# New durations and waits in a kernel's own list scheduler, and a stricter page allocator

## The chip, the cores and the metric

The kernel runs on one core of one Trainium2 chip. The metric is the device time of one execution in microseconds (us), lower being better. A core has five engines that work side by side, each through a queue of its own: the tensor engine (PE, whose weight loads the profile lists as PEld), the vector engine (DVE), the scalar engine (ACT), GpSimd (POOL) and the sync engine (SP), which here issues all DMA transfers. An engine takes its instructions in the order in which they were queued and waits on semaphores for the others.

## The reference

One inference step of a one-layer network, for 1024 prompt tokens and 32 sample tokens of width 1024, in float32:

```python
def layer(x, mk, mv, hg_s0, rw_s0, shift0, lb, lw):
    n = rmsnorm(x, lw['norm_mix'])
    p = n @ lw['w_in']
    hg_o, hg_s = hgrn2_mixer(p[..., :HG_COLS], lb, lw['hgrn_norm'], hg_s0)
    rw_o, rw_s, rw_shift = rwkv7_mixer(p[..., HG_COLS:], shift0, rw_s0, ...)
    x = x + jnp.concatenate([hg_o, rw_o], axis=-1) @ lw['w_out']
    x = x + cross_attend(rmsnorm(x, lw['norm_cross']), mk, mv, lw['w_cq'], lw['w_co'])
    n = rmsnorm(x, lw['norm_ffn'])
    x = x + (jax.nn.silu(n @ lw['w_ff1']) * (n @ lw['w_ff3'])) @ lw['w_ff2']
    return x, hg_s, rw_s, rw_shift
```

The HGRN2 mixer (4 heads of 128) and the RWKV-7 mixer (8 heads of 64) are recurrences over the tokens. The memory's keys and values, `rmsnorm(mem) @ w_k` and `@ w_v` for 256 memory tokens, are computed as well and returned, as are the states of the mixers. A last RMSNorm gives the outputs.

## The kernel before, in words

The 1056 tokens lie along the free dimension in three blocks of 352 (`TB`), the features on the partitions. Every weight and every activation of a dense product is split into two float32r parts, high and low; a product is the sum of three (high x high, high x low, low x high). `load_w` loads a column tile of a weight (128 x 1024, 512 KB), multiplies it by a norm's gain on DVE, and makes the parts, the high one on ACT and the low one on DVE or, for the mixers' projections, on POOL. `gemm` does the products of such a tile, 24 for each block of 352 tokens, into a bank of PSUM.

In the mixers (`mixers`, `rwkv`, `hgrn`) the tokens are worked through in segments of 256, in chunks of 64 or blocks of 32. There the products are small (64 or 128 columns, float32 or float16), and each piece is a long chain from engine to engine: PE, then ACT or DVE, then PE. `inverse`, which inverts triangular 64 x 64 matrices for RWKV-7, makes ACT copy float16 results between small products. The projections `x @ w_in` are the work that PE can do while such a chain is under way.

Nothing of this is issued as it stands in the code. Every call of an engine is recorded as a node of a graph by `Graph.record`, with edges from the reads and writes of the tiles, and a line of products on PE makes one node (`gemm` cuts it after six products). Then `Graph.order`, a list scheduler, plans all engines on the host while the program is built:

- `price` gives the time that a node takes on its engine and how much later its result can be used; `wait` gives the time from one engine's result to its use by another; `change` is added when PE goes from one node to another.
- A node's priority is the longest path of prices and waits from it to the end of the graph. A node may carry a bias that pushes it back (`BIAS`): the projections have it, so they fill in where nothing else is ready.
- For every engine a clock is kept. The engine that could start first gets, of its nodes whose operands are there by then and whose new tiles have a place (`fits`), the one with the longest path.
- `FIFO` names kinds of tiles that must be placed in the order of recording, and how many of each may live; `AHEAD` says how many units (an RWKV piece `rw`, its chain `rc`, an HGRN piece `hg`, a piece of attention `at`) may be under way at once; `LEAD` says when one of six phases may open.
- SBUF is given out in units of 66 words of a partition, in pages of 16 units, in five regions (`REGIONS`). "F" regions hold ordinary tiles, "R" regions float32r operands. In the mixers the regions f0, mb and ma (192, 192 and 64 units) are F, and hold all ordinary tiles, the projections' results among them. `place` looks for the place that is free the earliest; `fits` asks whether there is one; `take` gives it out. `RESERVE` units (64 in the mixers) are kept for the oldest node that is still to be issued.

The planned order is then issued as it is, engine by engine, and the hardware waits wherever a result is later than planned. The pick itself is this loop:

```python
for t, n in sorted(ready[e], key=lambda r: (max(r[0], now), -r[1].path)):
    t = max(t, now)
    if pick is not None and t >= pick[0]:
        break
    s = fits(n, t)
    if s is None:
        continue
    if pick is None or s < pick[0]:
        pick = s, n
    if s <= now:
        break
...
if e == "tensor":
    n.cost += change(last, n)
```

All instructions are issued from one line of `emit` (L337 in the profile), so the profile is read by the names of tiles. These are the regions: f, mb, ma are F regions (mb and ma become R later), r and wr hold float32r operands and raw weights, bank is PSUM.

## Time and profile before

| | |
|---|---|
| time, median of 3 runs | 2035.69 us (2035.36 to 2036.48) |
| profiled execution, span from first to last instruction | 2034.7 us |
| instructions | 36538 |
| busy: PE | 1954.2 us (96%), 14417 products |
| busy: DVE | 1101.1 us (54%) |
| busy: ACT | 801.0 us (39%) |
| busy: POOL | 622.5 us (31%) |
| DMA | 100.59 MB, mean 49 GB/s |

The profiled execution has its span as its own time; its device time isn't listed apart, and the median of the runs is 1.0 us above it. PE is busy nearly all the time, so the time is that of PE's products plus the idle time of PE plus what a lowered clock costs. The granted clock of PE is a share of its full speed: at 0.5 products take twice as long. A row of the table by stages has the length of the stretch, the busy time of each engine in it with its number of instructions, the granted clock, the share of the DMA engines and GB/s. A row of the waits says which engine waited, for whom, the total in us, how often, and the longest. A row of the groups has operation, tiles, shapes and number, then busy time in us and mean ns of one, then the idle time before.

### The profile page before, as it was taken

To read this page: it belongs to the slowest core of one execution; us is meant where nothing else is said; L and a number is where in the kernel's file an instruction comes from. 1 tells how busy PE (TensorE), PEld (TensorE's weight loads), DVE (VectorE), ACT (ScalarE), POOL (GpSimd) and SP (SyncE) were. 2 spreads that over 40 slices of the span, in tenths; PEclk is the share of its full clock that TensorE was granted. 3 is DMA by queue.
4 is the path that set the end of the run, shared out by engine and by line. 5 is a ranking of instruction groups with operands and counts; after the bars stand their busy time and mean duration, and the time that the engine had idled before them with its cause. 6 is when DMAs were issued, how large, how long until landed. Compare 5 with 4: busy or idle time off the path is not lost.

```text
span 2034.7 us, 36538 instructions
## 1 busy us (share of the span) xinstructions
PE 1954.2 (96%) x14417; PEld 1813.2 (89%) x14417; DVE 1101.1 (54%) x2584; ACT 801.0 (39%) x2066; POOL 622.5 (31%) x954
## 2 busy tenths in 40 slices
PE   7989999998999899899999999999999999999998
PEld 6878777787877788899989999999999999999997
DVE  4876677768767766635754356333333344323345
ACT  4576546845765676633332233121111112111122
POOL 4742343334434331206300056230022233310221
PEclk8999999998999999899999999999999999999999
DMA  4100100011010101541211111111211111111112
GB/s 139 42 22 25 35 23 27 23 34 33 22 32 18 33 23 58 179 147 42 73 42 42 42 53 42 42 40 40 59 50 39 40 58 42 50 40 53 46 42 86
DMA packets 159115, 100.59 MB, mean 49 GB/s; under 512 B 7776, under 2 KB 153824, under 8 KB 158944
## 3 DMA queue, kind: packets, MB, share of 16 engines
q1 hardware_dynamic: 158944, 98.26, 16.0%
q8 instruction: 113, 1.85, 0.4%
q14 instruction: 58, 0.48, 0.1%
HBM read 86.69 MB, written 11.55 MB: 48 GB/s over the span
## 4 chain that ended last, share of the span: by engine, by line
PE 59%; DVE 4%; POOL 1%; ACT 1%; issue 1%; DMA 1%; SPq 0%; DVEq 0%; ACTq 0%
PE bank L337 59%; DVE f L337 2%; ACT f L337 1%; POOL f L337 1%; DVE r L337 1%; POOL r L337 1%; DVE mb L337 0%; ACT mb L337 0%; DMA wr<-in_w_ck_dram 0%; ACT r L337 0%; DMA f<-mix_scratch 0%; DMA wr<-in_w_cq_dram 0%; DVE wr L337 0%; SPq L337 0%; POOL mb L337 0%
## 5 line engine op out<-in xcount | busy, mean ns | idle before, releaser
L337 PE MATMUL bank<-r 128*128 128x352 f32 x5904 | 1040.1, 331 | 12.4 <-POOL r L337 5.3
L337 PEld LDWEIGHTS bank<-r 128*128 128x128 f32 x5904 | 955.1, 190 | 27.6 <-POOL r L337 5.8
L337 DVE TENSOR_TENSOR f<-bank,f 128x256 f16<-128x256 f32 (+9 forms) x689 | 252.6, 391 | 355.4 <-PE bank L337 339.8
L337 PE MATMUL bank<-mb,r 128*128 128x352 f32 (+3 forms) x2448 | 411.5, 325 | 4.6 <-DVE r L337 2.5
L337 PEld LDWEIGHTS bank<-mb,r 128*128 128x128 f32 x2448 | 396.1, 188 | 9.5 <-DVE r L337 4.3
L337 POOL TENSOR_TENSOR f<-f 128x352 f32<-128x352 f32 (+6 forms) x242 | 198.2, 835 | 482.0 <-ACT f L337 459.4
L337 PE MATMUL bank<-f 128*128 128x64 f16 (+7 forms) x2612 | 291.6, 253 | 35.2 <-DVE f L337 15.7
L337 ACT CAST r<-wr 128x1024 fp32r<-128x1024 f32 (+2 forms) x154 | 145.1, 946 | 311.8 <-PE bank L337 298.1
L337 ACT ACTIVATE f<-f 128x256 f32<-128x256 f32 (+5 forms) x372 | 147.0, 411 | 245.9 <-DVE f L337 217.7
L337 PEld LDWEIGHTS bank<-f 128*128 128x128 f32 (+4 forms) x1564 | 163.6, 162 | 66.8 <-DVE f L337 16.9
L337 ACT COPY f<-f 64x256 f16<-64x256 f16 (+1 forms) x408 | 149.1, 367 | 46.1 <-DVE f L337 37.8
L337 DVE TENSOR_TENSOR r<-wr,r 128x1024 fp32r<-128x1024 f32 (+2 forms) x124 | 142.1, 1150 | 43.5 <-ACT r L337 43.3
L337 DVE TENSOR_TENSOR wr<-wr,f 128x1024 f32<-128x1024 f32 x82 | 105.8, 1292 | 104.5 <-DMA wr<-in_w_ff_dram 89.1
L337 POOL TENSOR_TENSOR r<-f,r 128x352 fp32r<-128x352 f32 x48 | 62.3, 1312 | 271.1 <-DVE f L337 216.9
L337 POOL TENSOR_SCALAR f<-f 128x64 f32<-128x64 f32 (+6 forms) x124 | 54.7, 442 | 159.2 <-DVE f L337 100.0
L337 DVE TENSOR_TENSOR ma<-bank,ma 128x352 f32<-128x352 f32 (+6 forms) x96 | 45.3, 486 | 94.6 <-PE bank L337 84.1
L337 PEld LDWEIGHTS <-f 128*128 128x128 f16 x1156 | 52.5, 99 | 35.6 <-issue 8.2
L337 POOL TENSOR_TENSOR r<-wr,r 128x1024 fp32r<-128x1024 f32 x30 | 71.7, 2393 | 29.5 <-ACT r L337 25.9
L337 ACT CAST mb<-f 128x352 fp32r<-128x352 f32 x66 | 30.9, 484 | 123.0 <-DVE f L337 114.7
L337 PE MATMUL bank<-f,mb 64*64 64x64 f32 (+7 forms) x830 | 75.3, 250 | 1.4 <-DVE f L337 1.1
L337 ACT ACTIVATE f<-bank,f 128x256 f32<-128x256 f32 (+4 forms) x122 | 51.1, 432 | 56.4 <-DVE f L337 19.7
L337 DVE TENSOR_TENSOR f<-bank,r 128x352 f32<-128x352 f32 x60 | 30.4, 518 | 77.0 <-PE bank L337 77.0
(167 smaller groups left out, 1770.6 us busy)
## 6 DMA issues: line engine op xcount, KB each, us to landing
wr<-in_w_ff_dram SPq DMA_DIRECT2D x44, 512.0 KB
wr<-in_w_in_dram SPq DMA_DIRECT2D x30, 512.0 KB
wr<-in_w_ff_dram SPq DMA_DIRECT2D x24, 384.0 KB
f<-mix_scratch SPq DMA_DIRECT2D x24, 176.0 KB
mb<-in_x_prompt_dram SPq DMA_DIRECT2D x16, 256.0 KB
wr<-in_w_ck_dram SPq DMA_DIRECT2D x8, 512.0 KB
wr<-in_w_cv_dram SPq DMA_DIRECT2D x8, 512.0 KB
wr<-in_w_out_dram SPq DMA_DIRECT2D x8, 512.0 KB
```

The lines of the kernel that those rows point to most:

```text
L337: getattr(eng, method)(*args, **kw)
```

## The change

It changes the planner alone; the recorded network is the same. `price` gets other durations, above all longer ones for ACT, POOL and DMA, longer ones for float32r products and other ones for small float32 products. `wait` becomes a table by producing and consuming engine. `change` is now 0.095 us wherever the size of the part of the array in use changes (rows up to 64 or not, columns up to 64 or not), and 0 elsewhere. `place` gets a rule: a node that isn't the oldest may not put an ordinary tile into an empty page where fewer than two pages are empty. `fits` now tries the places of all new tiles of a node one after the other, largest first, with the earlier ones taken, instead of each by itself. The tiles "raw" and "mixed" (the projection before and after the token shift in RWKV, 352 columns) come into `FIFO` with four live each. All comments and descriptions are removed as well.

```diff
-WAIT, WAIT_PE, SWITCH = 0.0, 0.1, 0.06
+SWITCH = 0.095
-FIFO = {"wr": 2, "wh": 2, "wl": 2, "p": 44, "h": 12, "rp": 5, "wr2": 4, "wh2": 8, "wl2": 8, "ckv": 7, "mrow": 2}
+FIFO = {"wr": 2, "wh": 2, "wl": 2, "p": 44, "h": 12, "rp": 5, "wr2": 4, "wh2": 8, "wl2": 8, "ckv": 7, "mrow": 2, "raw": 4, "mixed": 4}
...
+WAIT = {("vector", "tensor"): 0.2, ("vector", "gpsimd"): 0.18, "vector": 0.115, ("scalar", "tensor"): 0.1,
+        ("scalar", "gpsimd"): 0.05, "scalar": 0.02, ("gpsimd", "tensor"): 0.08, "gpsimd": 0.0, "tensor": 0.21,
+        ("sync", "tensor"): 0.08, "sync": 0.0}
 def wait(a, b):
-    if a == b:
-        return 0.0
-    if b == "tensor":
-        return 0.2 + WAIT_PE
-    return {"tensor": 0.2, "gpsimd": 0.08}.get(a, 0.14) + WAIT
+    return 0.0 if a == b else WAIT.get((a, b), WAIT[a])
 def price(eng, method, args, kw):
     if method == "dma_start":
-        return 0.45 + n * out.shape[0] * 4 / 380e3, 1.2
+        return max(0.4, n * out.shape[0] * 4 / 200e3), 1.9
     if eng == "tensor":
         if method == "transpose":
-            return (0.056 if args[1].shape[0] == 64 else 0.109), 0.0
+            return (0.056 if args[1].shape[0] <= 64 else 0.109), 0.0
         lhs = kw["lhsT"]
-        m = math.prod(lhs.shape[1:])
+        k, m = lhs.shape[0], math.prod(lhs.shape[1:])
         if lhs.dtype == F16:
-            return 0.029, 0.0
+            return max(0.029, n / 2400 + 0.002), 0.0
         if lhs.dtype == F32R:
-            return (n if n >= 256 else 4 * n) / 2400 + 0.002, 0.0
-        return (n / 790 if m == 64 else 4 * n / 2400 + 0.003), 0.0
+            return (n if n >= 256 else 4 * n) * 0.4375e-3 + 0.007, 0.0
+        if k <= 64 and m <= 64:
+            return max(0.03, n * 0.92e-3), 0.0
+        if k <= 64:
+            return max(0.112, n * 1.25e-3), 0.0
+        if m <= 64:
+            return (0.059 if n >= 64 else 0.112), 0.0
+        return max(0.223, n / 600 + 0.005), 0.0
     if eng == "vector":
         if method == "tensor_reduce":
             n = math.prod(args[1].shape[1:])
-        return 0.065 + n * 1.04e-3 + (0.065 if method in ("scalar_tensor_tensor", "tensor_tensor_scan") else 0.0), 0.0
-    if method == "affine_select":
-        return 0.3, 0.0
-    if method == "memset":
-        return 0.04 + n * 0.5e-3, 0.0
+        if method == "tensor_tensor_scan":
+            return 0.07 + n * 2.08e-3, 0.0
+        return 0.065 + n * 1.05e-3 + (0.065 if method == "scalar_tensor_tensor" else 0.0), 0.0
     if eng == "scalar":
-        return 0.095 + n * 0.83e-3 + (0.06 if any(isinstance(kw.get(k), View) for k in ("scale", "accum_out")) else 0.0), 0.0
+        pointer = any(isinstance(kw.get(k), View) for k in ("scale", "bias", "accum_out"))
+        return (0.18 if args[1].buf.space == "PS" else 0.21) + n * 0.83e-3 + (0.095 if pointer else 0.0), 0.0
+    if method == "affine_select":
+        return 0.35, 0.0
+    if method == "memset":
+        return 0.06 + n * 0.5e-3, 0.0
     if method == "tensor_tensor":
-        return 0.1 + n * 2.1e-3 + (0.45 if args[3] == ALU.pow else 0.0), 0.0
+        return 0.22 + n * 2.2e-3 + (0.45 if args[3] == ALU.pow else 0.0), 0.0
     if method == "tensor_scalar":
-        return 0.2 + n * (2.6e-3 if args[4] == ALU.max else 1.1e-3), 0.0
-    return 0.1 + n * 1e-3, 0.0
+        return 0.3 + n * (2.9e-3 if args[4] == ALU.max else 1.3e-3), 0.0
+    return 0.24 + n * 1e-3, 0.0
...
+def cut_of_array(call):
+    method, args, kw = call
+    op = args[1] if method == "transpose" else kw["lhsT"]
+    return op.shape[0] <= 64, method != "transpose" and math.prod(op.shape[1:]) <= 64
 def change(a, b):
-    if a is None:
-        return 0.0
-    (_, x, kx), (m, y, ky) = a.calls[-1], b.calls[0]
-    if m == "transpose":
-        full, half = y[1].dtype == F32, False
-    else:
-        full = ky["lhsT"].dtype != F16
-        half = math.prod(ky["lhsT"].shape[1:]) == 64
-    if math.prod(x[0].shape[1:]) > 64 or not full:
-        return 0.003
-    return 0.033 if half else SWITCH
+    return SWITCH if a is not None and cut_of_array(a.calls[-1]) != cut_of_array(b.calls[0]) else 0.0
...
-        def place(b, start):
+        def place(b, start, first):
             units = b.units
             step = 16 if units > 12 else 4 if units > 2 else units
             free = np.where(pages(b), freed, BIG)
             if units <= 16:
                 cand = free.reshape(-1, 16)
                 idle = (cand < BIG).sum(1)
+                if not first and b.kind == "F" and b.cls not in HOME and (idle == 16).sum() < 2:
+                    cand = np.where(idle[:, None] == 16, BIG, cand)
...
         def fits(n, start):
             first = n.i == oldest
...
-                for b in sb:
-                    if b.at is None:
-                        at = place(b, start)
-                        if at is None:
-                            return None
-                        start = max(start, at[1])
+                tried = []
+                for b in sorted(sb, key=lambda b: -b.units):
+                    at = place(b, start, first)
+                    if at is None:
+                        break
+                    start = max(start, at[1])
+                    lo, hi = at[0], at[0] + b.units
+                    tried.append((lo, hi, freed[lo:hi].copy()))
+                    freed[lo:hi] = BIG
+                for lo, hi, was in reversed(tried):
+                    freed[lo:hi] = was
+                if len(tried) < len(sb):
+                    return None
             return start
...
-                got = place(b, start)
+                got = place(b, start, n.i == oldest)
```

More of the change, by code (lines that the diff above doesn't have):

```diff
@@ L442, in place @@
                 idle = (cand < BIG).sum(1)
-                best = None
+                if not first and b.kind == "F" and b.cls not in HOME and (idle == 16).sum() < 2:
+                    cand = np.where(idle[:, None] == 16, BIG, cand)
                 offs = range(0, 17 - units, step)
```

## The prediction

> **What bounds the kernel now.** I read the table by stages first, cut where the kinds of work change: start, mixers, the step from the mixers to the output projection, and the dense products. Then came the waits of the tensor engine (PE) in the mixers.
>
> ```profile
> core 0: 2034.7 us, clock 0.978
> ```
>
> ```profile
> 0.00:100.00 100.00, 82.59 (x524) 76.00 (x526) 60.84 (x126) 51.59 (x125) 59.15 (x137) 0.91 0.29 92
> 100.00:800.00 700.00, 659.41 (x6400) 552.80 (x6397) 492.46 (x1468) 441.00 (x1293) 263.80 (x508) 0.97 0.10 28
> 800.00:1000.00 200.00, 187.70 (x1227) 180.38 (x1226) 115.06 (x206) 92.57 (x211) 67.54 (x82) 0.96 0.35 107
> 1000.00:2034.70 1034.70, 1024.48 (x6278) 1004.01 (x6277) 432.71 (x786) 215.89 (x440) 231.97 (x228) 1.00 0.16 49
> ```
>
> The columns after the length are busy time of PE, its weight loads, DVE, ACT and POOL, then the granted clock. PE is idle for 17.4, 40.6, 12.3 and 10.2 us, 80.5 us in all. The mean clock of 0.978 costs up to 0.022 x 2034.7 = 44.8 us more: 9 at the start (0.09 x 100), 21 in the mixers (0.03 x 700), 8 in the step (0.04 x 200). What an order can win is in these two sums. They overlap where PE stands idle at half clock, so 125 us is a ceiling. The dense half has little to give: one of its slices shows PE without a gap.
>
> ```profile
> 1300.00:1400.00 100.00, 100.00 (x623) 100.00 (x622) 33.67 (x50) 18.25 (x32) 26.05 (x24) 1.00 0.15 43
> ```
>
> That is 100 / 623 = 0.1605 us for one product of 352 columns. The old price is 352/2400 + 0.002 = 0.149 us, the new one 352 x 0.0004375 + 0.007 = 0.161 us. The new price is right, and the product stays as long as it was.
>
> Who ends the waits of PE in the mixers (total, number, longest):
>
> ```profile
> PE bank L337 <- DVE f L337: 14.5, 18, 2.5
> PE bank L337 <- ACT mb L337: 7.1, 9, 1.9
> PE bank L337 <- ACT f L337: 6.7, 12, 2.2
> PE bank L337 <- DVE mb L337: 4.6, 2, 4.2
> PE bank L337 <- DVE ma L337: 3.0, 2, 1.9
> PE bank L337 <- ACT ma L337: 2.3, 4, 1.1
> ```
>
> DVE ends 14.5 + 4.6 + 3.0 = 22.1 us, ACT 7.1 + 6.7 + 2.3 = 16.1 us. In these places the planner put a product in PE's queue before its operand was there, and everything behind it waits, since PE takes its products in order.
>
> **The change part by part.** No instruction is added or removed: the same products, copies and DMAs are put in another order and at other addresses. So the arithmetic costs the same, and only waits, the clock, and interference between engines can move. The new prices against the trace:
>
> ```profile
> L337 ACT COPY f<-f 64x256 f16<-64x256 f16 x320 | 128.0, 402 | 37.1 <-DVE f L337 30.2 <-POOL f L337 1.4
> L337 POOL TENSOR_TENSOR f<-f 128x352 f32<-128x352 f32 x138 | 148.4, 1100 | 391.1 <-ACT f L337 389.8
> L337 POOL TENSOR_TENSOR r<-wr,r 128x1024 fp32r<-128x1024 f32 x30 | 71.7, 2393 | 29.5 <-ACT r L337 25.9 <-PE bank L337 3.2
> L337 DVE TENSOR_TENSOR r<-wr,r 128x1024 fp32r<-128x1024 f32 x84 | 110.7, 1318 | 40.6 <-ACT r L337 40.5
> L337 DVE TENSOR_TENSOR f<-f,r 128x352 f32<-128x352 f32 x48 | 37.0, 784 | 1.0
> ```
>
> ACT's copy of 256 columns: old 0.307, new 0.422, traced 0.402. POOL's sum of 352: old 0.839, new 0.994, traced 1.100; its subtraction of 1024: old 2.250, new 2.473, traced 2.393. DVE's subtraction of 1024: old 1.130, new 1.140, traced 1.318; its sum of 352: old 0.431, new 0.435, traced 0.784. So ACT and POOL come to within a tenth, and DVE stays short by 14 to 45%.
>
> **ACT's waits** (16.1 us). A run of such copies was planned a quarter too short (0.307 for 0.402), so PE's operand came later than planned. With the new price the planner issues a projection product in the meantime, which is ready whenever its weights are. I take two thirds away, 10.7 us; a third stays since the allowance from ACT to PE falls as well, from 0.30 to 0.10. Bounds: all 16.1 gone, or 8 more.
>
> **DVE's waits** (22.1 us). The price is the old one, and the longest wait shows why it falls short. Rows of DVE, POOL and PE in order of time:
>
> ```profile
> 645.18 2.34 POOL L337 TENSOR_TENSOR r<-wr,r 128x1024 fp32r<-128x1024 f32 x1
> 645.25 2.48 DVE L337 TENSOR_TENSOR f<-mb,ma 128x192 f32<-128x192 f32 x1 [0.67 <-POOL mb L337]
> 648.41 0.97 PE L337 MATMUL bank<-mb 64*128 64x128 f32 x5 [4.25 <-DVE mb L337]
> ```
>
> A DVE operation priced at 0.065 + 192 x 0.00105 = 0.267 us lasts 2.48 us, as long as POOL's subtraction beside it. The Trainium skill, in "SBUF — State Buffer" under "Who interferes with whom", says that a DVE instruction with two SBUF inputs contends with a GpSimd instruction that reads SBUF, and that the second to issue blocks until the first has finished; this row agrees. No price by shape holds that, before or after. I take no change here. Bounds: half gone (-11) by the truer times of the other engines, or doubled (+22), by the rival below.
>
> **The clock.** One short wait and what followed:
>
> ```profile
> 145.60:147.50 1.90, 0.10 (x3) 0.05 (x2) 1.86 (x8) 0.00 (x0) 1.76 (x4) 1.00 0.00 0
> 151.20:158.10 6.90, 6.90 (x54) 5.35 (x55) 2.79 (x11) 1.58 (x4) 1.35 (x4) 0.51 0.00 0
> ```
>
> PE is busy for 0.10 of 1.90 us, and 3.7 us later runs 6.9 us at 0.51. So a wait costs clock as well: 21 / 40.6 = 0.52 us for each us of idle time in the mixers. With the 10.7 us go 5.5 us. The Trainium skill ("TensorE: Matmul & The Clock Gate", "What's actually happening") puts the throttle after at least one idle window of about 3.4 us. By that alone, the shorter waits would cost no clock and the 5.5 us would drop out of the sum; this row, a throttle after a wait of under 2 us, speaks for keeping them.
>
> **The step from mixers to output projection** (12.3 us idle). Here late loads stand in the chain that ended last:
>
> ```profile
> 861.85 5.77 DMA wr<-in_w_ck_dram
> 883.88 4.53 DMA f<-mix_scratch
> ```
>
> The waits of PE in this stage:
>
> ```profile
> PE bank L337 <- DVE f L337: 5.2, 4, 3.2
> PE bank L337 <- DVE r L337: 4.2, 5, 1.3
> PE bank L337 <- ACT mb L337: 1.8, 1, 1.8
> ```
>
> A weight of 512 KB was planned at 1.83 + 1.2 = 3.03 us and is now at 2.62 + 1.9 = 4.52; the traced piece is 5.77. The scratch load goes from 2.12 to 2.80, the piece is 4.53. Waits on r and mb behind such loads are 4.2 + 1.8 = 6.0 us; I take half away, 3.0 us, and with it clock at 8 / 12.3 = 0.65, 2.0 us. Bounds: all 6.0, or nothing. SP only issues these loads, which are no later in its queue for being priced higher.
>
> **The start** (17.4 us idle):
>
> ```profile
> PE bank L337 <- DMA f<-in_norm_mix_dram: 6.8, 1, 6.8
> PE bank L337 <- POOL r L337: 5.3, 2, 5.0
> PE bank L337 <- DVE mb L337: 3.2, 1, 3.2
> ```
>
> The first wait is for the first parameters and is not the planner's. The second is POOL's weight subtraction behind constants; its price hardly moves. I take nothing; bounds 5 less, 3 more.
>
> **Allocator and rest.** The exact trial of several tiles and the order imposed on "raw" and "mixed" (four live each) cost nothing while look-ahead has room. Free-kind SBUF in the mixers is 192 + 192 + 64 units, 28 pages of 16, and the rule keeps one empty page back from all but the oldest node. What hides it is the other 27; if that cover goes, it is a rival. The price of a switch (0.095) and the lower price of short products (0.059 for 0.081) move only the planner's clock, since the pick is made before the switch is added.
>
> The sum: 10.7 + 5.5 + 3.0 + 2.0 = 21.2 us less. The profiled span is 2034.7 us against a median of 2035.69, about 1 us outside it that stays. 2035.7 - 21.2 gives 2014.5, say 2014 us.
>
> **The rivals.**
>
> *More is won:* all ACT waits (16.1), half of DVE's (11), clock on both (27.1 x 0.52 = 14), the step (6 + 4), the start (5): 56 us, 1980 us. For it: every long wait is a planning error. Against it: DVE's price.
>
> *DVE's waits grow, slower.* The old planner allowed 0.30 us from any engine to PE, the new one 0.20 from DVE, so the cushion that covered a short DVE price shrinks by 0.10 us at each crossing, while PE's products are no longer priced short, which had given DVE time too. DVE has 1468 instructions in the mixers. If its waits double, 22.1 x 1.52 = 33.6 us come, less the 21.2 won: 2048 us. It decides from the point where DVE's waits pass 22.1 + 21.2 / 1.52 = 36 us. For it: DVE is the largest releaser, and its 784 ns sum is the worst-priced row. Against it: PE's operands also pass ACT, which now counts in full.
>
> *The allocator starves the look-ahead.* If projection results find no page, PE has no filler for the 20 RWKV pieces (4 pairs of heads, 5 segments). At 1 us each and clock on top, 30 us, less 21.2 x 0.5 kept: 2055 us. For it: the order was free before. Against it: no wait on a free page stands out among the rows above.
>
> *No change:* the priority by longest path to the end is as before, and PE is 94% busy in the mixers (659.41 of 700); the waits only move elsewhere: 2035.7 us.
>
> **How the numbers follow.** 0.2% is 4 us, about what a measurement of this kernel can tell from none. Forecast (2000 to 2031): 0.43. More won (about 1980): 0.17. No change: 0.06. DVE's waits grow: 0.22. Starved: 0.12. Faster is 0.43 + 0.17 = 0.60, same 0.06, slower 0.34. The range goes from 1984 to 2053: it leaves out about half of "more is won" and nearly half of the starved case with the tail of DVE's. The forecast's own range is 2000 to 2031.
>
> **What would show it.** Right: in the mixers ACT-ended waits near 5 us, DVE-ended ones near 22, PE idle near 30, clock about 0.975; in the step idle near 9; 0.16 us a product after it. Wrong: DVE-ended waits over 36 us, or granted clock below 0.97 in the mixers; or PE waits in the mixers for projection results whose weights had long been there, which would be the allocator.

## The result and the profile after

The changed kernel takes 2082.03 us (median of 4 runs, 2076.97 to 2084.31) against 2035.91 for the kernel before on the same chip. The ratio is 1.0238 (95% interval 1.0212 to 1.0263): 46 us slower, where 22 us faster had been forecast.

First the table by stages of the changed kernel, cut as in the prediction:

```profile
core 0: 2080.3 us, clock 0.962
...
0.00:100.00 100.00, 80.53 (x464) 74.74 (x466) 53.40 (x109) 48.32 (x118) 51.79 (x121) 0.93 0.30 92
100.00:800.00 700.00, 656.39 (x6268) 554.42 (x6266) 489.55 (x1427) 427.96 (x1236) 272.80 (x517) 0.94 0.09 27
800.00:1000.00 200.00, 174.08 (x1177) 159.88 (x1174) 97.79 (x229) 96.00 (x244) 50.46 (x71) 0.87 0.34 102
1000.00:2080.30 1080.30, 1064.84 (x6521) 1044.47 (x6519) 456.01 (x820) 231.29 (x466) 251.66 (x247) 1.00 0.16 48
```

PE is idle for 19.5, 43.6, 25.9 and 15.5 us, 104.5 in all (before 80.5). The mean clock of 0.962 costs up to 0.038 x 2080.3 = 79.1 us (before 44.8). The two overlap, since idle time at half clock costs nothing more.

A cut at round times hides where it happens. The next two tables are cut where the work changes: at the issue of the last projection product, and where both the mixers' last small product and the last product of the memory's keys and values are done. These two times come from laying each kernel's order beside its trace. First the kernel before:

```profile
100.00:804.00 704.00, 663.41 (x6426) 556.50 (x6423) 496.29 (x1480) 444.93 (x1305) 264.26 (x510) 0.97 0.10 28
804.00:881.00 77.00, 69.98 (x511) 65.46 (x510) 47.57 (x108) 48.47 (x122) 15.56 (x35) 0.89 0.55 171
881.00:2034.70 1153.70, 1138.20 (x6968) 1115.24 (x6966) 496.38 (x872) 256.05 (x517) 283.49 (x274) 1.00 0.17 51
```

Then the changed kernel:

```profile
100.00:806.00 706.00, 662.39 (x6315) 560.01 (x6314) 493.31 (x1437) 432.23 (x1248) 272.80 (x517) 0.94 0.09 27
806.00:927.00 121.00, 95.75 (x678) 82.33 (x677) 64.05 (x175) 69.65 (x191) 19.85 (x43) 0.79 0.43 133
927.00:2080.30 1153.30, 1137.17 (x6967) 1116.42 (x6966) 486.00 (x866) 253.37 (x509) 282.27 (x274) 1.00 0.16 49
```

The last part takes 1153.7 and 1153.3 us, the first 704 and 706. So 44 us are lost in the middle, in the hand-over from the mixers to the output projection (77 to 121 us), and it is two things. The changed kernel enters it with more work left: 678 products to do in place of 511, because by the last projection it had done fewer: 60 fewer in the first 100 us (464 for 524), and 111 fewer in the mixers in the same busy time, at a clock of 0.94 for 0.97. And it does them with PE idle for 25.2 us in place of 7.0, at a clock of 0.79 for 0.89. By the mean clock of the stretch, an estimate, the busy times at full clock would be 95.75 x 0.79 = 75.6 and 69.98 x 0.89 = 62.3 us. Of the 44 us, then, about 13 are work left over, 18 are idle time, and 12 are clock lost while busy (20.1 against 7.7). The waits of PE in this stretch, before:

```profile
PE bank L337 <- DVE f L337: 5.2, 4, 3.2
PE bank L337 <- DVE r L337: 0.9, 1, 0.9
```

And after:

```profile
PE bank L344 <- DVE f L344: 10.1, 11, 2.5
PE bank L344 <- DMA f<-out_dram: 5.1, 1, 5.1
PE bank L344 <- ACT f L344: 4.1, 2, 3.5
PE bank L344 <- ACT r L344: 3.2, 1, 3.2
```

Two kinds of waits grew: those for the mixers' chains (DVE f, ACT f), and those of the memory itself, for the parts of its weights (ACT r) and for its results being read back (DMA f<-out_dram).

What fills PE in that stage? The products with 256 columns from r and ma are those of the memory's keys and values, 384 of them. They hang on no mixer, so they can run while a mixer's chain is under way in other engines. Groups of PE by form, kernel before, from the last projection to the mixers' last small product:

```profile
L337 PE MATMUL bank<-r,ma 128*128 128x256 f32 x361 | 50.4, 297 | 0.9 <-DVE r L337 0.9
```

The changed kernel, from the last projection to the mixers' last small product at 875 us, and from there to 927:

```profile
L344 PE MATMUL bank<-r,ma 128*128 128x256 f32 x84 | 14.3, 325 | 0.0
...
L344 PE MATMUL bank<-r,ma 128*128 128x256 f32 x301 | 40.2, 295 | 5.2 <-ACT r L344 3.2 <-DVE r L344 2.0
```

Before, nearly all of them lay beside the mixers' tail; after, 84 did, and the other 300 came when the mixers were over. The mixers' tail took nearly as long with so few of them, though with more small products of its own (806 to 875, before 804 to 878), so some 50 us behind it were added.

The waits of PE in the mixers (100 to 800 us), after:

```profile
PE bank L344 <- DVE f L344: 20.0, 26, 3.2
PE bank L344 <- DVE ma L344: 8.2, 10, 1.9
PE bank L344 <- ACT f L344: 8.1, 8, 4.9
PE bank L344 <- DVE mb L344: 3.0, 5, 1.6
PE bank L344 <- ACT ma L344: 2.2, 3, 1.2
```

ACT now ends 10.3 us of waits (before 16.1), DVE 31.2 (before 22.1).

### The profile page after: what moved, and what is told of

The parts are those of the page before. It is cut to its first block, busy times and chain, and to the rows that moved or that the text cites. A ratio compares the mean times of both kernels' runs of the same rounds, so it can differ in the third digit from the quotient of the medians.

```text
span 2080.3 us, 36540 instructions
## 1 busy us (share of the span) xinstructions
PE 1975.8 (95%) x14417; PEld 1833.5 (88%) x14417; DVE 1096.8 (53%) x2584; ACT 803.6 (39%) x2064; POOL 626.7 (30%) x954
## 4 chain that ended last, share of the span: by engine, by line
PE 77%; DVE 9%; POOL 3%; ACT 3%; issue 2%; DMA 1%; SPq 0%; DVEq 0%; ACTq 0%; POOLq 0%
PE bank L344 77%; DVE f L344 6%; ACT f L344 2%; POOL f L344 2%; DVE mb L344 1%; DVE ma L344 1%; POOL r L344 1%; DMA wr<-in_w_cv_dram 1%; ACT r L344 0%; DVE r L344 0%; ACT ma L344 0%; DMA out_dram<-f 0%; DMA f<-mix_scratch 0%; POOL mb L344 0%; ACT mb L344 0%
## 5 line engine op out<-in xcount | busy, mean ns | idle before, releaser
L344 DVE TENSOR_TENSOR f<-bank,f 128x256 f16<-128x256 f32 (+6 forms) x702 | 257.1, 392 | 369.1 <-PE bank L344 349.2
L344 PE MATMUL bank<-f 64*64 64x64 f32 (+8 forms) x2545 | 299.7, 263 | 45.9 <-DVE f L344 19.6
L344 POOL TENSOR_TENSOR f<-f 128x352 f32<-128x352 f32 (+7 forms) x244 | 197.3, 827 | 482.0 <-ACT f L344 457.3
L344 ACT ACTIVATE f<-f 128x256 f32<-128x256 f32 (+6 forms) x375 | 149.1, 410 | 257.0 <-DVE f L344 213.8
L344 PEld LDWEIGHTS bank<-f 64*64 64x64 f32 (+3 forms) x1623 | 171.0, 166 | 83.1 <-DVE f L344 21.0
L344 DVE TENSOR_TENSOR r<-wr,r 128x1024 fp32r<-128x1024 f32 (+2 forms) x124 | 136.9, 1109 | 66.6 <-ACT r L344 66.5
L344 ACT COPY f<-f 64x256 f16<-64x256 f16 (+1 forms) x340 | 125.4, 370 | 61.3 <-DVE f L344 51.1
L344 POOL TENSOR_SCALAR f<-f 128x64 f32<-128x64 f32 (+6 forms) x109 | 54.3, 500 | 149.9 <-DVE f L344 76.7
L344 PE MATMUL bank<-f,mb 64*64 64x64 f32 (+7 forms) x758 | 79.5, 269 | 5.5 <-DVE f L344 3.4
L344 PEld LDWEIGHTS bank<-f,mb 64*64 64x64 f32 (+5 forms) x758 | 60.4, 163 | 19.6 <-DVE f L344 5.3
```

The source lines that it names most:

```text
L344: getattr(eng, method)(*args, **kw)
```

## The experiments

The theories:

- **A, the filler.** The time is lost because the memory's products no longer lie beside the mixers' tail.
- **B, the mixers.** It is lost by new waits and a lower clock inside the mixers, which the new prices order badly.
- **C, the draw.** A list scheduler's order changes as a whole with any nudge. The kernel before held an unusually good order, and the change gave an ordinary one.
- **D, the planner.** The new prices, waits or allocator are themselves worse.
- **E, the better planner.** The new planner is the better one once luck is taken out.

All runs in one table. "Tail" is the time from the last projection to the end of mixers and memory products, "left" the small products still to be issued at its start, "memory" those of the 384 memory products that come before the mixers' last small product, and "rest" the time from the tail's end to the end of the span. These come from each run's trace and order; ratio and interval are to the kernel before as run beside them, whose median was 2032 to 2033 us for all kernels below the second row; distances in the text are to that. The positions belong to the one profiled execution, which can lie some us off the median of its kernel.

| kernel | time, us | ratio (95%) | last projection at | left | memory | tail | rest |
|---|---|---|---|---|---|---|---|
| before | 2035.91 | 1 | 803.6 | 113 | 360 | 77.0 | 1154.1 |
| after | 2082.03 | 1.0238 (1.0212 to 1.0263) | 806.3 | 268 | 84 | 119.8 | 1154.2 |
| b_lead150 | 2071.90 | 1.0202 (1.0187 to 1.0217) | 800.5 | 113 | 108 | 118.2 | 1152.2 |
| b_one | 2009.02 | 0.9887 (0.9872 to 0.9901) | 803.7 | 113 | 96 of 96 | 56.8 | 1147.9 |
| a_one | 2037.16 | 1.0027 (1.0015 to 1.0039) | 806.3 | 268 | 96 of 96 | 76.7 | 1152.5 |
| oldact | 2056.23 | 1.0123 (1.0108 to 1.0138) | 820.7 | 113 | 324 | 81.6 | 1152.2 |
| a_rows | 2067.91 | 1.0173 (1.0156 to 1.0191) | 807.3 | 268 | 252 | 109.6 | 1150.0 |
| jb_act1 | 2109.33 | 1.0380 (1.0358 to 1.0403) | 786.4 | 580 | 132 | 165.7 | 1152.2 |
| jb_dve2 | 2059.10 | 1.0127 (1.0105 to 1.0148) | 828.9 | 113 | 336 | 81.4 | 1147.6 |
| oldall3 | 2088.74 | 1.0278 (1.0260 to 1.0297) | 776.2 | 688 | 228 | 160.3 | 1151.5 |
| draw_old1 | 2083.40 | 1.0260 (1.0221 to 1.0299) | 810.7 | 113 | 324 | 88.3 | 1181.5 |
| draw_old2 | 2089.78 | 1.0280 (1.0257 to 1.0303) | 811.6 | 106 | 288 | 84.8 | 1189.7 |
| draw_new1 | 2095.82 | 1.0319 (1.0282 to 1.0356) | 761.6 | 520 | 180 | 148.3 | 1178.3 |
| draw_new2 | 2096.48 | 1.0323 (1.0302 to 1.0344) | 794.1 | 207 | 48 | 116.3 | 1183.2 |
| mix_old1 | 2067.04 | 1.0163 (1.0146 to 1.0180) | 793.3 | 266 | 168 | 120.0 | 1152.1 |
| mix_old2 | 2078.86 | 1.0227 (1.0208 to 1.0247) | 814.8 | 113 | 288 | 103.6 | 1151.6 |
| mix_new1 | 2084.11 | 1.0245 (1.0220 to 1.0270) | 814.9 | 141 | 84 | 108.6 | 1152.2 |
| best_new | 2025.45 | 0.9960 (0.9946 to 0.9975) | 795.9 | 113 | 324 | 71.9 | 1151.0 |
| top_new | 2032.49 | 1.0006 (0.9992 to 1.0021) | 800.0 | 123 | 324 | 79.7 | 1149.6 |
| top_old | 2044.99 | 1.0058 (1.0035 to 1.0081) | 814.0 | 113 | 360 | 77.8 | 1155.6 |

### Open the memory's phase later, in the kernel before

```diff
-LEAD = {0: BIG, 1: 1100, 2: 250, 3: 400, 4: 300, 5: 40}
+LEAD = {0: BIG, 1: 150, 2: 250, 3: 400, 4: 300, 5: 40}
```

> One constant of the kernel before: phase 1 (the memory rows, keys and values) opens when 150 nodes of phase 0 are left instead of 1100. Costs, waits and pages stay the old ones. Theory A (filler): the 46 us were lost because the memory keys' and values' 384 products, 45 us of TensorE time, came after the mixers' small products instead of between them. Then this kernel loses like the changed one: 2065 to 2075 us, with most of the memory products behind the mixers' last small product, and a stage from the last mixer projection to the first output projection of 105 to 120 us in place of 77. Theory B (the mixers' waits): the loss comes from new waits and a lower clock inside the mixers' chains, which the new costs ordered badly. Then this kernel, whose mixers keep the old order, stays at 2034 to 2042 us.

Measured: 2071.9 us, 40 more than before. The table by stages:

```profile
100.00:800.00 700.00, 661.75 (x6397) 555.28 (x6396) 487.99 (x1463) 437.17 (x1282) 264.99 (x507) 0.97 0.09 25
800.00:919.00 119.00, 80.15 (x524) 72.82 (x523) 57.59 (x131) 60.63 (x150) 14.62 (x37) 0.78 0.47 149
919.00:2070.90 1151.90, 1137.84 (x6968) 1115.15 (x6966) 491.95 (x866) 252.03 (x510) 283.48 (x274) 1.00 0.16 49
```

And its waits of PE from 800 to 919 us:

```profile
PE bank L337 <- DVE f L337: 21.5, 3, 9.5
PE bank L337 <- ACT r L337: 11.1, 4, 10.2
```

The mixers are as good as before up to the last projection (700 us at 0.97, 4 us less than before), the same 113 small products are left, and the tail still grows from 77 to 118 us. PE waits for chains (DVE f) that nothing covers, and then for the memory weights' parts (ACT r). Theory A's mechanism is shown, and for this order its size: the later place of the memory's phase costs about 40 us. The edit moves the whole phase, rows and weights with the products, so part of it is the weights' parts coming late. And it doesn't yet say how much of the change's 46 us is of this kind.

### Take three quarters of the filler away, in both kernels

```diff
-        for h in range(4):
+        for h in range(1):
...
-                    kt, val = memory(self.mk[:, :, h], self.mv[:, :, h])
+                    kt, val = memory(self.mk[:, :, 0], self.mv[:, :, 0])
```

> The kernel before with a quarter of the memory keys and values: it computes them for head 0 alone (96 products in place of 384) and the attention reads head 0's for all four heads, so the outputs of the other three heads are not the reference's. It is to be read with its twin, the changed kernel with the same cut. Theory A (filler): beside the mixers' tail these products cost little, so taking 288 of them away (34 us of busy time) brings 3 to 10 us: 2026 to 2033 us. Theory B (the mixers' waits): the products cost their busy time in both kernels alike: about 2002 to 2010 us.

> The changed kernel with the same cut: memory keys and values for head 0 alone, read for all four heads. Theory A (filler): in this kernel the 288 products stood behind the mixers with nothing beside them, so the cut brings their whole time, 34 to 42 us: 2040 to 2048 us, and the distance to the twin of the kernel before falls from 46 us to 10 to 20. Theory B (the mixers' waits): the distance to the twin stays at 40 to 50 us.

Measured: 2009.0 and 2037.2 us. The cut brings some 43 us to the changed kernel (1.0238 to 1.0027), just over theory A's 34 to 42, but 23 to the kernel before, where A expected 3 to 10; its 2009 us lies in theory B's range. The distance falls from 46 to 28 us, neither A's 10 to 20 nor B's 40 to 50. The hand-over of the kernel before with the cut, and then of the changed kernel with it:

```profile
804.00:861.00 57.00, 41.06 (x255) 35.18 (x254) 34.63 (x97) 33.06 (x98) 15.31 (x35) 0.83 0.33 103
```

```profile
806.00:883.00 77.00, 63.11 (x423) 51.98 (x421) 47.65 (x156) 49.83 (x160) 21.49 (x43) 0.75 0.30 91
```

Theory A had the filler nearly free in the kernel before, and it wasn't: without three quarters of it the mixers' last small product ends at 861 us in place of 878, and the tail takes 57 us in place of 77. The start of the output projection doesn't set the two apart: both begin it while the mixers end, at 831 and at 872 us, and issue 36 of its products before the mixers' last small product. What remains of the distance lies for the most part in the tail, 56.8 against 76.7 us: the changed kernel has 268 small products left there, the other 113. So the change did two things, the memory came late, and the mixers were further behind when the projections ran out. By this pair the first is worth some 20 us (43 less 23), half of what b_lead150 gives, and 28 us remain.

### Undo one price

```diff
-        return (0.18 if args[1].buf.space == "PS" else 0.21) + n * 0.83e-3 + (0.095 if pointer else 0.0), 0.0
+        return 0.095 + n * 0.83e-3 + (0.06 if pointer else 0.0), 0.0
```

> The changed kernel with one price undone: the activation engine's instructions cost the old 0.095 us + 0.83 ns an element again; the other prices, the waits and the page allocator are the new ones. The order that comes out of it has 27 of the 32 groups of memory products before the mixers' last small product (the changed kernel 7, the kernel before 30). Theory A (filler): 2034 to 2045 us, the stage behind the last mixer projection back at 75 to 90 us. Theory B (the mixers' waits): the new waits and the allocator are what costs, and this kernel stays above 2065 us. A third, that the activation engine's price itself orders the mixers badly, gives 2035 to 2045 as well, but with the gain inside the mixers (clock up from 0.94, fewer waits) and the stage behind them unchanged at 115 to 125 us.

Measured: 2056.2 us, which none of the three had.

```profile
100.00:821.00 721.00, 669.77 (x6468) 561.16 (x6465) 496.96 (x1481) 441.57 (x1291) 270.40 (x523) 0.96 0.09 27
821.00:902.00 81.00, 69.53 (x515) 64.93 (x513) 51.53 (x120) 53.49 (x138) 15.73 (x36) 0.89 0.48 152
```

The tail is back at 81 us with 324 memory products in it, as A says, but the stretch to the last projection is 17 us longer than before. Undoing one price gave a whole new order, good at the tail and bad in the mixers. This run suggested that single edits of this planner can't be read as the price of the edit, and led to theory C.

### Prepare the memory's rows earlier, in the changed kernel

```diff
+        bias, nc.bias = nc.bias, 0.0
         rs = self.load_rows([(self.i["mem_prompt"]...
+        nc.bias = bias
```

> The changed kernel with one more edit: the preparation of the memory's rows is no longer pushed behind the projections (its bias is 0). The order of the tensor engine stays that of the changed kernel up to about the last projections; then 21 of the 32 groups of memory products come before the mixers' last small product, in place of 7. Theory A (filler): 2058 to 2070 us, and the stage from the last mixer projection to the end of mixers and memory products at 95 to 108 us in place of 121. Theory B (the mixers' waits and clock): no change from the changed kernel's 2082 (2078 to 2086).

Measured: 2067.9 us, some 13 less than the changed kernel (1.0238 to 1.0173), as A expected; the tail of 110 us is just over its 95 to 108.

```profile
100.00:807.00 707.00, 664.28 (x6303) 561.20 (x6303) 492.36 (x1435) 432.43 (x1248) 273.14 (x516) 0.94 0.09 27
807.00:917.00 110.00, 88.09 (x676) 78.18 (x674) 62.95 (x174) 68.25 (x189) 18.66 (x43) 0.86 0.44 141
```

The first row is the changed kernel's (706 us, 662.39, clock 0.94). With 252 memory products beside the tail in place of 84, the tail is 110 us in place of 120. So in the changed kernel the bias, which puts the memory's rows behind the projections, keeps back more than half of the missing filler. But with that back only 13 of the 46 us return; PE is still idle for 21.9 of the 110 us.

### A nudge that means nothing

```diff
-        return 0.095 + n * 0.83e-3 + (0.06 if any(...) else 0.0), 0.0
+        return 0.096 + n * 0.83e-3 + (0.06 if any(...) else 0.0), 0.0
```

> The kernel before with a price changed by 1 ns (an instruction of the activation engine costs 0.096 us + 0.83 ns an element in place of 0.095), which is nothing beside the 95 to 100 ns by which the traces differ from the old price. The order that comes out is another one nearly from the start: 11 of 32 groups of memory products beside the mixers (before 30) and 381 small calls left when the last projection is issued (before 73). Theory C (the order is a draw: any nudge gives another one, and the kernel before held a good one): 2055 to 2085 us. Theory D (the changed prices and allocator themselves cost the 46 us): 2030 to 2045 us, as the prices are the old ones.

```diff
-        return 0.065 + n * 1.04e-3 + ...
+        return 0.065 + n * 1.045e-3 + ...
```

> A second nudge of the kernel before: DVE's element costs 1.045 ns in place of 1.04. The order is again another one, but this one has 28 of 32 groups of memory products beside the mixers and 73 small calls left behind the last projection, like the kernel before. If the hand-over decides (theory A): 2032 to 2048 us with the stage behind the last projection at 75 to 85. If the order inside the mixers varies as much (as in the kernel with the old activation price, where the mixers lost 17 us): 2045 to 2062 us, with that stage at 75 to 85 all the same. Theory D: 2030 to 2045 us.

Measured: 2109.3 and 2059.1 us. One nanosecond on one price of the kernel before costs 77 us, more than the whole change. Tables by stages, the 1 ns kernel first:

```profile
100.00:786.00 686.00, 636.98 (x5951) 535.82 (x5950) 473.38 (x1344) 406.33 (x1163) 247.05 (x481) 0.95 0.09 27
786.00:952.00 166.00, 125.54 (x988) 106.06 (x987) 87.73 (x250) 94.80 (x268) 27.50 (x63) 0.75 0.32 100
```

The DVE nudge:

```profile
100.00:829.00 729.00, 675.53 (x6400) 565.13 (x6399) 500.06 (x1465) 439.83 (x1284) 258.61 (x508) 0.95 0.09 27
829.00:910.00 81.00, 68.60 (x516) 63.85 (x515) 52.70 (x121) 54.30 (x140) 17.23 (x36) 0.92 0.52 163
```

They lose it in the two ways already seen. The 1 ns kernel issues the projections too early (the last at 786 us with 580 small products left), and the chains that remain have too little beside them: 166 us at 0.75. The other keeps a good tail and loses 25 us ahead of it. Theory D, which had both at 2030 to 2045, falls as an explanation of differences of this size; theory C stands, its range for the first still too low.

### The allocator alone

The empty-page rule, the exact trial and the two FIFO entries stay; `price`, `wait` and `change` are the old ones.

> The allocator half of the change alone: the rule for empty pages, the exact trial of several tiles and the order of raw and mixed are in, while prices, waits and the switch are the old ones. 19 of 32 groups of memory products come beside the mixers, but 447 small calls are left behind the last projection. Theory D with the prices as the cause: 2030 to 2045 us. Theory D with the allocator as the cause: 2070 to 2085 us, with waits for projection results inside the mixers. Theory C: 2055 to 2080 us, the loss read from the stage behind the last projection (over 100 us in place of 77), with no wait that the allocator explains.

Measured: 2088.7 us, 56 more than before.

```profile
100.00:776.00 676.00, 632.54 (x5889) 534.23 (x5890) 462.10 (x1337) 395.97 (x1146) 251.55 (x479) 0.95 0.09 27
776.00:937.00 161.00, 131.79 (x1099) 112.28 (x1098) 97.94 (x274) 101.78 (x292) 33.38 (x76) 0.76 0.33 102
```

Its picture is that of the 1 ns nudge: projections used up at 776 us, 688 small products left. As a meaningless nudge costs 77 us, these 56 can't be charged to the allocator.

### Ordinary orders of both planners

To take the luck out, at most 10 ns were added to each node's priority, by a fixed pattern; of some 35 patterns for each planner those in the middle by the planner's own end were run. Two patterns are for the old planner and two for the new one.

```diff
+        for n in nodes:
+            n.path += (n.i * 10) % 101 * 1e-4
```

> The kernel before with at most 10 ns added to each node's priority (path), by a fixed arithmetic pattern that means nothing; prices, waits and allocator are the old ones. Of 37 such patterns this is the one in the middle by the planner's own end. 27 of 32 groups of memory products come beside the mixers. Theory C (the kernel before holds a draw far better than its planner's usual one): 2070 to 2115 us. Theory D (the new prices and allocator cost the 46 us): within 10 us of the kernel before, 2025 to 2045.

> A second draw from the middle for the old planner (another pattern of at most 10 ns on the priorities, 24 of 32 groups of memory products beside the mixers). Theory C: 2070 to 2115 us. Theory D: 2025 to 2045 us.

> The changed kernel with such a pattern on the priorities (at most 10 ns); the one in the middle, by the planner's own end, of 35 that could be built (15 of 32 groups of memory products beside the mixers, 325 small calls left behind the last projection). Theory C: the changed kernel is a good draw of its planner too, so 2085 to 2125 us, and the middle draws of the old and the new planner lie within 15 us of each other. Theory E (the new prices are better once the luck of the draw is taken out): 2040 to 2075 us, at least 20 below the old planner's middle draws. Theory D: 2075 to 2090 us, some 46 above the old planner's.

> A second draw from the middle for the new planner (4 of 32 groups of memory products beside the mixers, 122 small calls left behind the last projection). Theory C: 2085 to 2125 us. Theory E: 2040 to 2075 us. Theory D: 2075 to 2090 us.

Measured: 2083.4 and 2089.8 us with the old planner, 2095.8 and 2096.5 with the new one, all as theory C had it; theory D, which had the old planner's at 2025 to 2045, and theory E, in the form that the new planner's ordinary order is 20 us or more under the old one's, fall. But part of it was not foreseen: the rest, about 1152 us in the other kernels, took 1178 to 1190 here. Stretch of draw_old1 from its FFN to the end, and its waits from there:

```profile
1264.00:2080.50 816.50, 785.06 (x4831) 768.56 (x4829) 308.58 (x477) 142.76 (x264) 183.85 (x191) 1.00 0.16 47
...
PE bank L337 <- DVE r L337: 19.1, 22, 1.1
```

The pattern also reaches the nodes of the dense half, where it presumably breaks ties among equal ones, and PE waited 22 times for the low part of a weight (DVE r). The same products take 29 us less in the kernel before:

```profile
1247.00:2034.70 787.70, 778.51 (x4829) 772.43 (x4827) 307.12 (x477) 144.85 (x264) 186.00 (x190) 1.00 0.16 48
```

So the runs were repeated with the pattern on the mixers' nodes alone:

```diff
+        for n in nodes:
+            if n.phase == 0:
+                n.path += (n.i * 166) % 101 * 1e-4
```

> The kernel before with a pattern of at most 10 ns on the priorities of the mixers' nodes alone; the one in the middle of 25 by the planner's own end (14 of 32 groups of memory products beside the mixers). The dense half keeps its order, so from the end of mixers and memory products on it should take the 1150 to 1154 us of the kernel before. Theory C (the old planner's ordinary order is as slow as the changed kernel): 2062 to 2088 us. Theory D (the new prices and allocator cost the 46 us): 2030 to 2045 us. Half and half: 2045 to 2062 us.

> A second pattern on the mixers' nodes alone, next to the middle (24 of 32 groups beside the mixers). Theory C: 2060 to 2085 us. Theory D: 2030 to 2045 us. Half and half: 2045 to 2060 us.

> The changed kernel with a pattern on the mixers' nodes alone, next to the middle of the 20 that could be built (7 of 32 groups beside the mixers, as in the changed kernel). Theory C: the changed kernel is an ordinary draw of its planner, so 2070 to 2095 us, within 15 us of the old planner's two. Theory D: 2075 to 2090 us, 40 or more above them.

Measured: 2067.0 and 2078.9 us with the old planner, 2084.1 with the new one; the rest is 1152 us in all three, so the 26 to 38 us more of the first four came from the dense half's nodes. Two ordinary orders of the old planner are 1.6% and 2.3% slower than the kernel before, and the changed kernel and another ordinary order of the new planner 2.4% and 2.5%. Both old orders lie in theory C's ranges and 20 us or more above theory D's; the new one lies in its ranges by both theories, 5 and 17 us above the old two, where C had said within 15 and D 40 or more. The kernel before was a rare order of its planner: of 25 patterns on the mixers' nodes none ended as early by the planner's own reckoning, and the best of the 57 behind top_old below comes to the same planned end. Read so, most of the 46 us, 34 to 46 by these two runs, is the loss of that order. This rests on two orders of one planner. Between the planners 0.47% remains by the mixers' patterns (mean ratio 1.0242 for the two new orders, 1.0195 for the two old ones) and 0.51% by the first set, about 10 us. The two old orders differ by 12 us themselves, so this is a hint and not settled.

### The best order of each planner

The changed kernel with the early memory rows of a_rows and a pattern on the mixers' nodes, the best of 11 by the planner's own end:

> The changed kernel with the memory's rows prepared early (bias 0) and the best of 11 patterns on the mixers' nodes by the planner's own end: 27 of 32 groups of memory products beside the mixers, 73 small calls left behind the last projection. Theory A with C: 2042 to 2060 us, well under the changed kernel and still above the kernel before, whose mixers are the quicker ones. If the hand-over were all (theory A alone): 2030 to 2042 us.

Measured: 2025.5 us beside 2033.1 for the kernel before, a ratio of 0.9960 (0.9946 to 0.9975): quicker than both kernels, and below both ranges expected.

```profile
100.00:796.00 696.00, 658.45 (x6482) 556.38 (x6479) 493.48 (x1498) 447.69 (x1314) 272.46 (x527) 0.97 0.10 29
796.00:868.00 72.00, 65.14 (x504) 60.87 (x503) 47.82 (x105) 48.19 (x116) 14.28 (x33) 0.95 0.56 176
```

Both stages are better than before, in an execution of 2020.5 us, 5 under the median: 696 us for 6482 products (before 704 for 6426), 72 us for the tail (before 77). Groups of PE in its tail:

```profile
L344 PE MATMUL bank<-r,ma 128*128 128x256 f32 x384 | 51.0, 289 | 0.3 <-DVE r L344 0.2
```

The products run from the last projection on, with a wait of 0.3 us in all. The distance to the kernel before is 0.4%, clear of the spread of these runs, but of one order, picked from 11. Then the best of a longer search on each side, with the early rows in both:

> The changed kernel with the memory's rows prepared early (bias 0) and the best of 82 patterns on the mixers' nodes by the planner's own end (27 of 32 groups beside the mixers, 78 small calls left behind the last projection). Theory E (the new prices make the better orders once one is picked by the planner's own end): 2012 to 2030 us, under the kernel before. If best_new was luck: 2035 to 2060 us.

> The kernel before with the memory's rows prepared early (bias 0) and the best of 57 patterns on the mixers' nodes by the planner's own end, which comes to the same planned end as the kernel before (30 of 32 groups, 73 small calls). Theory E: 2030 to 2050 us, no better than the kernel before and at least 10 above the best of the new planner. If the planners are alike in their best draws: 2012 to 2030 us.

Measured: 2032.5 us, the same as the kernel before within 0.2%, and 2045.0. The new planner's pick, the best of 82, is quicker than the old one's, the best of 57, by 0.5%, as theory E says. But it isn't under the kernel before, which E also said, and best_new, which the planner puts behind it, is 7 us quicker. The order top_old has the planned end of the kernel before and is 12 us slower. The planner's own end picks among its orders, but not to a few us. So theory E is neither shown nor excluded by these orders.

## Why the prediction was wrong

**The ceiling** and where the time can go (idle time of PE and clock) were the right columns; all of the loss is in them.

**ACT's waits:** forecast -10.7 us, measured 16.1 to 10.3, -5.8. The sign was right and the size half, inside the bounds given (8 more to 16.1 less).

**DVE's waits:** forecast no change, measured 22.1 to 31.2, +9.1. It stays below the 36 us from which the rival would decide, and idle time in the mixers rose by 3.0 us (40.6 to 43.6) where 10 less were expected. The rival "DVE's waits grow" had the sign of these waits and of the result, not the place of the loss: by its price of 1.52 us, 9.1 us of waits come to 14 us of the 46.

**The clock:** forecast 0.975 in the mixers, measured 0.94, below the 0.97 named as the sign of error. At 0.06 x 700 it costs 42 us in place of 21. Here the step that failed is the rate of 0.52 us for each us of idle time: 43.6 us of idle time now go with 42 us. The last projection is issued only 3 us later, so this loss reaches the total as the products that weren't done by then.

**The step from the mixers to the output projection:** forecast 5 us less, measured 44 more. This is the main failure. The prediction priced the late loads in it and took for granted that what fills PE there stays where it was. It counted the transfers of the stage, and not the 361 products that made its 77 us possible. In b_lead150, moving the memory's phase costs 40 us with the mixers as they were; by b_one and a_one its place makes some 20 of the 46, and the small products left over are the other part.

**The start** kept its idle time within the bounds (17.4 us forecast unchanged, 19.5 measured), but 60 fewer products were done in it, which no term held. The product of 352 columns (forecast 0.16 us) held: the dense part takes the same time in both kernels to 0.4 us. That no instruction is added or removed holds for the products; ACT has 2064 instructions in place of 2066, two table loads fewer.

**Allocator and rest:** forecast at nothing. No run settles it. The allocator alone came out 56 us slower, by a tail like that of the 1 ns nudge. The rival by which it starves the look-ahead is therefore neither shown nor excluded.

**What stood behind all of it:** each edit was priced as if the order stayed and only its waits shrank. No rival said that the order is drawn anew, and that the one at hand was far better than its planner's usual one. That could have been read beforehand as a question: the hand-over lived on one arrangement (361 products beside the tail, 7.0 us idle in 77) that no price in the planner protects. The 0.34 for slower stood on DVE's waits and the allocator alone, and both of their prices (2048 and 2055 us) lie below the 2082 measured.

**Open:** how the 46 us divide between the late memory and the mixers left behind; the runs give 13 (a_rows, with part of the filler back), 20 (b_one and a_one) and 40 us (b_lead150) for the first. Why the memory's products come later in so many orders of the new planner than of the old one. Two things were seen, the bias of the memory's rows (a_rows, worth 13 us) and the region "ma", which holds their operands and must first be empty of the mixers' tiles; the second was not tried alone and is read from the code. Nor is it settled whether the new prices cost or gain a few us for themselves.

## What to carry to other kernels

In a kernel whose order comes from a list scheduler, first nudge a constant by a nanosecond and measure: that spread, here 1.3% to 3.8% slower, is the noise against which an edit of the planner must be read, by several orders on each side. Then look at where the filler ends and the chains do not: here the largest losses lay at the hand-over, and went with how much independent work and how many links of the chains were still there when the last projection was issued. They are not the only ones: oldact and jb_dve2 kept a good hand-over and lost 17 and 25 us ahead of it. And a planner that is cheap to run should be asked for many orders, the best few of which are measured.

## What the runs showed of the hardware

The clock falls in fixed pieces. In the mixers of the kernel before (100 to 804 us) the trace records 8 stretches at half clock, 47.8 us together; in the changed kernel (100 to 806) 11 of 85.3 us. All are multiples of 3.41 us: 14 and 25 pieces, so that each piece costs up to 1.7 us. One such stretch in the changed kernel:

```profile
557.10:560.60 3.50, 2.89 (x43) 2.19 (x42) 2.25 (x7) 3.33 (x10) 2.22 (x3) 1.00 0.38 102
560.60:564.40 3.80, 3.80 (x26) 3.26 (x27) 2.36 (x6) 2.86 (x8) 0.32 (x1) 0.54 0.15 44
564.40:567.80 3.40, 3.40 (x23) 2.80 (x23) 0.76 (x3) 1.84 (x5) 0.00 (x0) 0.50 0.02 5
```

PE was busy for 2.89 of 3.50 us, idle for 0.61, and the next two pieces ran at half clock though PE had no gap in them. The Trainium skill ("TensorE: Matmul & The Clock Gate", "What's actually happening") gives a free-running window of 3413 ns, which agrees with the pieces; it puts the throttle after at least one idle window, and here a piece with PE busy for 83% was followed by it. That is the highest share; the other stretches in the mixers of the two kernels followed pieces with PE busy for 6% to 75%. The prediction's row, cut into such pieces:

```profile
144.41:147.82 3.41, 1.61 (x19) 1.34 (x20) 3.32 (x11) 0.84 (x2) 2.30 (x5) 1.00 0.00 0
147.82:151.23 3.41, 2.42 (x32) 1.82 (x27) 2.48 (x9) 0.61 (x2) 2.15 (x4) 1.00 0.02 5
151.23:158.06 6.83, 6.83 (x54) 5.31 (x54) 2.75 (x11) 1.58 (x4) 1.32 (x4) 0.50 0.00 0
```

The wait lies in the first piece, with PE busy for 1.61 us, and yet the second still has the full clock; half clock comes behind that one, with PE busy for 2.42 us. So the busy share of the piece just before doesn't decide it alone, and the runs don't show what does. They do show that a rate per us of idle time doesn't hold: in the mixers of the two kernels, 40.6 and 43.6 us of idle time went with 47.8 and 85.3 us at half clock.
